# A hybrid encoder layer on one core: V's class transfers issued by ScalarE, and the product groups that stand beside the attention spread anew

## The chip, the core and the metric

The kernel runs on 1 core of one Trainium2 chip. The metric is the device time of one execution in microseconds (us), smaller being better. Inside a core, TensorE (PE) multiplies matrices into PSUM, VectorE (DVE) and ScalarE (ACT) do elementwise work, GpSimd (POOL) does small work and issues some transfers, and SyncE (SP) issues most transfers. Each engine takes its instructions in order; an instruction that waits holds up all that stand behind it on its engine.

## The reference

One layer with sequence 512 and width 1024, all in float32. Two head groups share one input projection: a gated linear recurrence (RG-LRU, forward and backward) and attention with three dilated windows. Cut to what matters here:

```python
h = rms_norm(x, attn_norm_g[l])
xr, gate, q, k, v = split(h @ w_in[l])              # 5 x 512 columns
y_rnn = (rg_lru(xr, fwd) + rg_lru(xr, bwd)) * gelu(gate)
y_attn = dilated_attention(q, k, v, rel_bias)       # 8 heads of 64; windows (128,1), (512,4), (2048,16)
mix = concat([rms_norm(y_rnn, g1), rms_norm(y_attn, g2)])
x = x + mix @ w_out[l]
x = x + square(relu(rms_norm(x, g3) @ w_up[l])) @ w_down[l]
return rms_norm(x, final_norm_g)
```

## The kernel before, in words

Every large product is made of three matmuls in a reduced float32 format (`mm3`, L311): the high part of the weights with the high and the low part of the data, and the low part of the weights with the high part of the data. A **group** below is one `mm3` over a contraction of 128. Weights come in chunks of 512 KB into three buffers (`wraw`). For each chunk ACT makes the high part (`conv_hi`, L260) and DVE the low part (`conv_lo`, L268); the low part frees the buffer, and `emit_dma` (L243) asks SP for the next chunk. In the Q and K products `feed_q` does this for the chunk three ahead, the high part at contraction step k = 1 and the low part at k = 5.

The order of work on PE, ACT, DVE and POOL is written out by hand: it is the order of the program. Only SP's order is found by the framework, from readiness in its own model.

The stages that matter here: V is projected early and stays in PSUM; ACT writes it to SBUF during the gate products (`v_evac`, L717). `v_far(j)` (L722) then copies V from SBUF to SBUF in another order, by classes of positions modulo 4: five transfers in all, 256 KB each but two of 128 KB, from 128 partitions into 32 (16) each. The result `vc` is read by `att_av`, first at the end of step 1.

Then comes the attention: five steps i = 0 to 4, each of four quarters u = 0 to 3. Step i treats head pair p = i (i < 4) and finishes pair i - 1:

- `att_s(i, 0)` and `att_s(i, 2)`: scores on PE, near (`pn`, L777) and far (`pf`, L784). The near ones have two PSUM buffers, so `att_s(i, 2)` waits until DVE has read those of quarters 0 and 1. Scores need `qraw` (L749), `kraw` (L753) and, for the far ones, `kfar`, K rearranged by ACT (`k_far`, L757).
- `att_f` (L797) and `att_e` (L816, L819): bias and minimum on DVE, exponential on ACT.
- `att_t` (L831, L833): transposes on PE, evacuated by ACT; `att_r`: the same for the reciprocal denominators.
- `att_av(i - 1)` (L912): the product with V at the end of the step, evacuated by DVE (`yp`, L928), then squared on ACT and added on DVE (`att_y`, L588).

Between these pieces stand **fillers**, groups of other products, taken in order from a queue by `fill(n)`: first 48 groups for K and Q of pairs 1 to 3 (8 for K, 8 for Q of each pair), then `load_x`, then 32 groups of the recurrence half of the output projection (`wo_thunks`, `pwo<-whi,yh`). Six are taken ahead of step 0 (`PRE`), then `FILL[(i, u)]` says how many at each of the four places of a quarter, four in all where it has no entry. `plan` hangs further pieces of ACT and DVE work on such places (`beside(i, u, place)`).

`load_x` reuses the two buffers of the normed input, so it starts when the last K or Q group is done. It loads the residual `x1` and four sums of blocks of w_out (`ws`): a plain load by SP (L1001) and then accumulating loads by POOL (L1003), each of which waits for the one before on the same sum.

Behind step 4: `att_av(3)`, `att_y(3)`, a few fillers, the column sums of the squares (`col_sums`, L411), `rv` (DVE, L396), `rcol`, the reciprocal root (POOL, L399), the remaining fillers, and the attention half of the output projection by a seven-product scheme of half blocks (`wo_m`, `pwo<-whi,oh`, in the order of `OSEQ`), whose results DVE scales by `rcol` and adds to `x1` (`wo_x`, L1120). The recurrence half is evacuated by DVE in L967. The up and down projections follow and take the larger part of the time.

Of the kernel before, what the change touches and what calls it, by code (L numbers as in the profile page):

```python
# [108 lines left out]
def hybrid_kernel(ctx: ExitStack, tc, xw, xn, w_in, w_v, w_out, w_up, w_dn, gates, vecs, rel, onehot, fg, out):  # L109
    nc = tc.nc  # L110
# [12 lines left out]
    def g_(name, dt=FT, shape=(P, S)):  # L123
        return work.tile(list(shape), dt, name=name, tag="g", bufs=NG)
# [4 lines left out]
    def ps_(name, tag):  # L129
        return psum.tile([P, S], FT, name=name, tag=tag, bufs={"pj": 4, "gs": 2, "et": 2}[tag])  # L130
# [122 lines left out]
    def conv_hi(i):  # L253
        if i < len(chunks):
            i = swap.get(i, i)
            hi = stream.tile([P, 1024], FR, name="whi", tag="whi", bufs=4)
            if i in ON_DVE:
                nc.vector.tensor_copy(hi, raws[i])
            else:
                act(hi, raws[i], AF.Copy)  # L260
            splits[i] = (hi,)

    def conv_lo(i):
        if i < len(chunks):
            i = swap.get(i, i)
            r = raws.pop(i)
            lo = stream.tile([P, 1024], FR, name="wlo", tag="wlo", bufs=4)
            nc.vector.tensor_tensor(lo, r, f(splits[i][0]), op=OP.subtract)  # L268
            splits[i] += (lo,)
            c = chunks[i]  # L270
            if isinstance(c, tuple) and c[0] == "o":
                if c[1][0] != "s":
                    emit_dma()
            elif isinstance(c, tuple) and len(c) == 4:
                h, kind, f0 = c[:3]
                if kind == "t1" and cq[h, f0, "t2"] not in raws:
                    nc.gpsimd.dma_start(r, ublock(h, "22", f0), accum_op=OP.add)
                    raws[cq[h, f0, "t2"]] = r
                elif kind == "22":
                    t = raws[cq[h, f0, "t3"]]  # L280
                    nc.vector.tensor_tensor(t, t, r, op=OP.add)
                elif kind in ("t2", "21"):
                    held[kind] = r
                    if len(held) == 2:
                        t = held.pop("t2")
                        nc.vector.tensor_tensor(t, t, held.pop("21"), op=OP.add)
                        raws[cq[h, f0, "t4"]] = t
                        emit_dma()
                if kind in ("11", "22"):
                    emit_dma()  # L290
            elif isinstance(c, tuple) and c[1][0] == "s":
                nxt = {"s1": ("s2", "22"), "s2": ("s4", "21")}.get(c[1])
                if nxt:
                    nc.gpsimd.dma_start(r, wblock(c[0], nxt[1], c[2]), accum_op=OP.add)
                    raws[cd_[c[0]] + {"s2": 2 * NQ + 2 * c[2], "s4": 6 * NQ + c[2]}[nxt[0]]] = r
            else:
                emit_dma()
# [7 lines left out]
    def feed_q(c, k):  # L305
        if k == 1:
            conv_hi(c + 3)
        elif k == 5:
            conv_lo(c + 3)

    def mm3(o, a, b, first, last, on=False):  # L311
        nc.tensor.matmul(o, lhsT=a[0], rhs=b[0], start=bool(first), stop=False, skip_group_check=on)  # L312
        nc.tensor.matmul(o, lhsT=a[0], rhs=b[1], start=False, stop=False, skip_group_check=on)  # L313
        nc.tensor.matmul(o, lhsT=a[1], rhs=b[0], start=False, stop=bool(last), skip_group_check=on)  # L314
# [60 lines left out]
    def hk(k):  # L375
        return (h_hi[:, k, :], h_lo[:, k, :])

    def wk(c, k):
        if c < 3:
            return tuple(t[:, c * P:(c + 1) * P] for t in w3[k])  # L380
        hi, lo = splits[c]
        return (hi[:, k * P:(k + 1) * P], lo[:, k * P:(k + 1) * P])
# [144 lines left out]
    def lru_gelu(t):  # L527
        act(gt[t], gt[t], AF.Gelu_apprx_tanh)
# [182 lines left out]
    vs, vc = vb[:, 0:4, :], vb[:, 4:8, :]  # L711
# [7 lines left out]
    def v_far(j):  # L719
        for a, b, s in (((0, P, 32 * j - 16),) if j else ((0, 64, 112), (64, P, 0))):  # L720
            n = (b - a) // 4
            nc.sync.dma_start(vc[s:s + n], vs[a:b, j, :])  # L722

    last = [scan_ops_end(t) for t in range(4)]

# [29 lines left out]
    def k_far(p):  # L755
        t = raw[p, 2] = g_("kfar")
        act(t.rearrange("p (c s) -> p s c", c=4), raw[p, 1].rearrange("p (s c) -> p s c", c=4), AF.Copy)  # L757
# [82 lines left out]
    def att_z(p):  # L840
        rz = small("rz", 8)
        nc.vector.reciprocal(rz, zs.pop(p))
        rzb = g_("rzb")
        nc.vector.tensor_copy(rzb, fan(rz, 0, 8, DH))
        rzbs[p] = rzb

    def att_r(p):
        rzb = rzbs.pop(p)
        pr = rows_of(lambda tt: rzb[:, tt * P:(tt + 1) * P], "et")
        zrow[p] = g_("zrow")  # L850
        act(zrow[p], pr, AF.Copy)
# [81 lines left out]
    def q_thunks(p, is_k, tag="pj"):  # L933
        c = C_QK + 2 * p + 1 - is_k
        o = {}

        def mk(k):
            def run():
                if k == 0:
                    o["p"] = ps_("pqk", tag)  # L940
                mm3(o["p"], wk(c, k), hk(k), k == 0, k == KD - 1)
                feed_q(c, k)
                if k == KD - 1:
                    (k_evac if is_k else q_evac)(p, o["p"])
            return run
        return [mk(k) for k in range(KD)]
# [23 lines left out]

    for n, th in enumerate(q_thunks(0, 1) + q_thunks(0, 0)):
        th()
        if n == 8:
            k_far(0)
        if n % 4 == 0:
            lru_gelu(n // 4)
    fillers = deque()

    def fill(n):
        for _ in range(n):  # L980
            if fillers and fillers[0] is None:
                fillers.popleft()
                load_x()
            if fillers:
                fillers.popleft()()
# [25 lines left out]
    def hi(t):  # L1011
        return lambda: y_hi(t, yrnn[t])

    def lo(t):
        return lambda: y_lo(t, yrnn.pop(t))

    def end(t):
        return lambda: rnn_end(t)

    def sq_(t):  # L1020
        return lambda: rnn_sq(t)
# [4 lines left out]
    def op(fn, *a):  # L1026
        return lambda: fn(*a)


    plan = {(0, 0, 0): [end(0)], (0, 0, 2): [sq_(0), add], (0, 0, 3): [end(1)],  # L1030
            (0, 1, 1): [sq_(1)],
            (0, 2, 3): [add],
            (1, 0, 2): [end(2)],
            (1, 1, 0): [sq_(2)], (1, 1, 2): [end(3)], (1, 1, 4): [add],
            (1, 3, 0): [sq_(3)], (1, 3, 2): [hi(0)], (1, 3, 3): [add, hi(1)], (2, 0, 2): [rnn_cols],
            (2, 0, 0): [lo(0), lo(1)], (2, 0, 4): [hi(2)],
            (2, 1, 2): [hi(3)], (2, 1, 4): [lo(2)], (2, 2, 3): [lo(3)]}
    for i in range(3):
        plan.setdefault((i, 1, 0), []).append(lambda p=i + 1: k_far(p))

    def beside(*key):
        for e in plan.pop(key, ()):
            e()
# [5 lines left out]
    for key, fs in (((4, 0, 4), [(o_sum, "s1", 0), (o_sum, "s2", 0), (o_sum, "s3", 0), (o_sum, "s3", 1)]),  # L1049
# [2 lines left out]
                    ((4, 2, 0), [(o_hi, "s3", 0), (o_hi, "s3", 1)]), ((4, 2, 2), [(o_lo, "s3", 0), (o_lo, "s3", 1), (o_sum, "22", 0)]),  # L1052
                    ((4, 2, 4), [(o_hi2, 0)]), ((4, 3, 0), [(o_lo2, 0), (o_hi, "s1", 0)]), ((4, 3, 4), [(o_lo, "s1", 0), (o_hi, "22", 0), (o_lo, "22", 0)])):
        plan[key] = [op(*a) for a in fs]
    FILL = {(3, 1): (1, 1, 1, 0), (3, 2): (1, 1, 1, 0), (3, 3): (1, 1, 1, 0), (4, 0): (0, 1, 0, 0), (4, 1): (0, 1, 0, 1), (4, 2): (0, 1, 0, 0), (4, 3): (0, 0, 0, 1)}


    for i in range(5):
        for u in range(4):
            if i == 0:  # L1060
                v_far(u)
            if i < 4 and u in (0, 2):
                att_s(i, u)
                if i < 3:
                    load_tw(2 * i + 2 + u // 2)
            if i >= 1 and u < 3:
                att_t(2 * i - 2, "abc"[u])
                att_t(2 * i - 1, "abc"[u])
            if i < 4:
                if u < 2:  # L1070
                    att_f(i, 2 * u)
                    att_f(i, 2 * u + 1)
                att_e(i, u)
            if u == 0 and i >= 1:
                att_z(i - 1)
            beside(i, u, 0)
            fill(FILL.get((i, u), (1, 1, 1, 1))[0])
            beside(i, u, 1)
            fill(FILL.get((i, u), (1, 1, 1, 1))[1])
            if u == 1 and i >= 1:  # L1080
                att_r(i - 1)
            if u == 0 and i >= 2:
                att_y(i - 2)
            beside(i, u, 2)
            fill(FILL.get((i, u), (1, 1, 1, 1))[2])
            beside(i, u, 3)
            fill(FILL.get((i, u), (1, 1, 1, 1))[3])
            beside(i, u, 4)
            if u == 3 and 1 <= i < 4:
                att_av(i - 1)  # L1090
    assert not plan
# [43 lines left out]
    def h2_l(k):  # L1135
        nc.vector.tensor_tensor(hb["l"][:, k, :], hm[k], f(hb["h"])[:, k, :], op=OP.subtract)

    fill(1)
    att_av(3)
    att_y(3)  # L1140
    fill(4)
    cs = col_sums(ssy[1], "gs")
    rc[1] = rstd_cols(cs, S)
    o_sum("s1", 1)
# [17 lines left out]
    for w in OSEQ:  # L1162
        for i in range(4):
            tt, k = (i % 2, i // 2) if w == "s2" else (i // 2, i % 2)
# [253 lines left out]
    for half in range(2):  # L1418
# [202 lines left out]
        if half == 1:  # L1621
            b = 6 * NQ
# [87 lines left out]
```

## Time and profile before

| | us |
|---|---|
| median of 3 runs | 538.83 (537.76 to 539.11) |
| the profiled execution | 539.04 |
| its span | 537.2 |
| PE busy | 524.9 |
| DVE busy | 423.3 |
| ACT busy | 352.2 |
| POOL busy | 64.0 |

The span is the time from the first to the last instruction of the profiled execution; 1.8 us lie around it. In a row of the timeline the columns are the start, the duration, the engine and its line, the operation, the output and the inputs, and the count; a bracket holds the idle time of the engine just before and what ended it. The ends of matmuls are modelled, so PE's rows overlap. The attention runs from 97.9 us to the column sums at 187.3 us; the up projection begins at 212.8 us.

### The profile page before, as it was taken

How to read it: one execution, taken by the hardware profiler on the slowest of the kernel's cores; microseconds unless marked ns; L12 is line 12 of the kernel's file. 1: busy time of each engine (PE TensorE's matmuls, PEld its weight loads, DVE VectorE, ACT ScalarE, POOL GpSimd, SP SyncE). 2: the span in 40 equal slices, each digit the busy share in tenths (PEclk: the TensorE clock that was granted, in tenths of full speed). 3: DMA queues.
4: the chain of work that ended last, by engine and by line, in shares of the span. 5: the costliest groups of instructions: out<-in, count | busy, mean ns of one | idle time of the engine just before them, and what ended most of it. 6: DMA issues, size and time to landing. Idle time of an engine off the chain costs nothing.

```text
span 537.2 us, 9162 instructions
## 1 busy us (share of the span) xinstructions
PE 524.9 (98%) x3507; PEld 448.3 (83%) x3507; DVE 423.3 (79%) x695; ACT 352.2 (66%) x557; POOL 64.0 (12%) x91
## 2 busy tenths in 40 slices
PE   8999999899999999999999999999999999999995
PEld 6866888687887778889999888888999999888884
DVE  6897787776674799889769987879756987987885
ACT  7677957567845745586576755566657686655664
POOL 3330000000001130001030213001001110131000
PEclk9999999999999999999999999999999999999998
DMA  7754068642299688856586799995888496799704
GB/s 276 210 161 141 32 171 182 183 114 70 90 298 307 165 166 203 285 193 180 166 177 177 195 252 274 288 356 116 282 235 206 117 220 193 174 301 263 174 0 157
DMA packets 34587, 104.10 MB, mean 194 GB/s; under 512 B 3981, under 2 KB 6954, under 8 KB 34544
## 3 DMA queue, kind: packets, MB, share of 16 engines
q1 hardware_dynamic: 26304, 74.66, 41.2%
q0 software_dynamic: 7920, 28.61, 28.5%
q8 instruction: 27, 0.44, 0.4%
q10 hardware_dynamic: 320, 0.25, 0.1%
q14 instruction: 16, 0.13, 0.1%
HBM read 96.15 MB, written 4.21 MB: 187 GB/s over the span
## 4 chain that ended last, share of the span: by engine, by line
PE 75%; DMA 10%; ACT 5%; DVE 5%; issue 2%; POOL 1%; SPq 0%; DVEq 0%; ACTq 0%; POOLq 0%
PE pu L314 10%; PE pu L313 10%; PE pu L312 10%; PE pd L312 9%; PE pd L314 9%; PE pd L313 9%; DMA ws<-in_w_out_dram 6%; DMA wraw<-in_w_in_dram 3%; PE pqk L312 2%; PE pqk L313 1%; PE pqk L314 1%; PE pg L502 1%; PE pxr L312 1%; PE pxr L314 1%; PE pxr L313 1%
## 5 line engine op out<-in xcount | busy, mean ns | idle before, releaser
L268 DVE TENSOR_TENSOR wlo<-wraw,whi 128x1024 fp32r<-128x1024 f32 x73 | 88.9, 1221 | 28.3 <-ACT whi L260 28.1
L260 ACT ACTIVATE whi<-wraw 128x1024 fp32r<-128x1024 f32 x70 | 74.0, 1059 | 44.6 <-PE pd L314 20.5
L313 PE MATMUL pd<-wlo,ah 128*128 128x512 f32 (+1 forms) x195 | 75.2, 386 | 0.0
L312 PE MATMUL pd<-whi,ah 128*128 128x512 f32 (+1 forms) x195 | 75.2, 386 | 0.0
L314 PE MATMUL pd<-whi,al 128*128 128x512 f32 (+1 forms) x195 | 75.2, 386 | 0.0
L313 PE MATMUL pu<-hl,whi 128*128 128x256 f32 x224 | 63.4, 283 | 0.0
L314 PE MATMUL pu<-hh,wlo 128*128 128x256 f32 x224 | 63.4, 283 | 0.0
L312 PE MATMUL pu<-hh,whi 128*128 128x256 f32 x224 | 63.4, 283 | 0.0
L260 ACT ACTIVATE whi<-tw 128x1024 fp32r<-128x1024 f32 x36 | 38.1, 1060 | 37.0 <-DMA tw<-in_w_up_dram 10.1
L314 PE MATMUL pu<-h2h,wlo 128*128 128x256 f32 (+1 forms) x200 | 60.1, 301 | 0.2 <-DVE wlo L268 0.2
L312 PE MATMUL pu<-h2h,whi 128*128 128x256 f32 (+1 forms) x200 | 60.1, 300 | 0.0
L313 PE MATMUL pu<-h2l,whi 128*128 128x256 f32 (+1 forms) x200 | 60.0, 300 | 0.0
L268 DVE TENSOR_TENSOR wlo<-tw,whi 128x1024 fp32r<-128x1024 f32 x36 | 44.0, 1222 | 17.5 <-ACT whi L260 17.5
L312 PEld LDWEIGHTS pu<-hh,whi 128*128 128x128 f32 x224 | 43.0, 192 | 0.0
L313 PEld LDWEIGHTS pu<-hl,whi 128*128 128x128 f32 x224 | 43.0, 192 | 0.0
L314 PEld LDWEIGHTS pu<-hh,wlo 128*128 128x128 f32 x224 | 43.0, 192 | 0.0
L314 PEld LDWEIGHTS pd<-whi,al 128*128 128x128 f32 x195 | 36.6, 188 | 7.4
L313 PEld LDWEIGHTS pd<-wlo,ah 128*128 128x128 f32 x195 | 36.6, 188 | 7.4
L312 PEld LDWEIGHTS pd<-whi,ah 128*128 128x128 f32 x195 | 36.6, 188 | 7.2
L260 ACT ACTIVATE whi<-ts 128x1024 fp32r<-128x1024 f32 x24 | 25.5, 1061 | 24.3 <-PE pd L314 18.1
L314 PEld LDWEIGHTS pu<-h2h,wlo 128*128 128x128 f32 x200 | 38.3, 191 | 1.8 <-DVE wlo L268 0.6
L312 PEld LDWEIGHTS pu<-h2h,whi 128*128 128x128 f32 x200 | 38.3, 191 | 1.3
(265 smaller groups left out, 1222.6 us busy)
## 6 DMA issues: line engine op xcount, KB each, us to landing
wraw<-in_w_up_dram SPq DMA_DIRECT2D x25, 512.0 KB
ts<-in_w_dn_dram POOLq DMA_DIRECT2D x24, 512.0 KB, 13.6
wraw<-in_w_dn_dram SPq DMA_DIRECT2D x24, 512.0 KB
tw<-in_w_up_dram SPq DMA_DIRECT2D x15, 512.0 KB
tw<-in_w_up_dram POOLq DMA_DIRECT2D x15, 512.0 KB, 7.4
wraw<-in_w_in_dram SPq DMA_DIRECT2D x13, 512.0 KB
ts<-in_w_dn_dram SPq DMA_DIRECT2D x8, 512.0 KB
tw<-in_w_dn_dram SPq DMA_DIRECT2D x8, 512.0 KB
```

The source lines that it names most:

```text
L260: act(hi, raws[i], AF.Copy)
L268: nc.vector.tensor_tensor(lo, r, f(splits[i][0]), op=OP.subtract)
L312: nc.tensor.matmul(o, lhsT=a[0], rhs=b[0], start=bool(first), stop=False, skip_group_check=on)
L313: nc.tensor.matmul(o, lhsT=a[0], rhs=b[1], start=False, stop=False, skip_group_check=on)
L314: nc.tensor.matmul(o, lhsT=a[1], rhs=b[0], start=False, stop=bool(last), skip_group_check=on)
L502: nc.tensor.matmul(pg[2 * d + j][halves[b ^ d]], lhsT=gwr[t][halves[b], c], rhs=xc[t][halves[b]], start=True, stop=True)
```

## The change

`v_far` issues its transfers on ACT's queue in place of SP's, and in step 0 it is called at the end of each quarter in place of its beginning. `k_far(p)` is called by the third Q group of its pair, in place of fixed places (the ninth group of the first pair's products, and the second quarter's start of steps 0 to 2).

The filler table changes. Steps 0 to 2 take 14 groups each (4, 3, 4, 3 by quarter) in place of 16; step 3 takes 12 in place of 13; step 4 takes 8 in place of 5. So the 48 K and Q groups end with step 2, where before six groups of the output projection had been taken by then. 20 of the 32 groups of the output projection are taken by the end of step 4, before 24. None is now taken between step 4 and `att_av(3)`, before one; five stand between `att_y(3)` and the column sums, before four; and seven behind them, before three.

```diff
     def v_far(j):
         for a, b, s in (((0, P, 32 * j - 16),) if j else ((0, 64, 112), (64, P, 0))):
             n = (b - a) // 4
-            nc.sync.dma_start(vc[s:s + n], vs[a:b, j, :])
+            nc.scalar.dma_start(vc[s:s + n], vs[a:b, j, :])
...
                 mm3(o["p"], wk(c, k), hk(k), k == 0, k == KD - 1)
                 feed_q(c, k)
+                if k == 2 and not is_k:
+                    k_far(p)
...
     for n, th in enumerate(q_thunks(0, 1) + q_thunks(0, 0)):
         th()
-        if n == 8:
-            k_far(0)
...
-    for i in range(3):
-        plan.setdefault((i, 1, 0), []).append(lambda p=i + 1: k_far(p))
...
-    FILL = {(3, 1): (1, 1, 1, 0), (3, 2): (1, 1, 1, 0), (3, 3): (1, 1, 1, 0), (4, 0): (0, 1, 0, 0), (4, 1): (0, 1, 0, 1), (4, 2): (0, 1, 0, 0), (4, 3): (0, 0, 0, 1)}
+    FILL = {(i, u): (1, 1, 1, 1 - u % 2) for i in range(3) for u in range(4)}
+    FILL.update({(3, u): (1, 1, 1, 0) for u in range(4)})
+    FILL.update({(4, u): (0, 1, 0, 1) for u in range(4)})
...
     for i in range(5):
         for u in range(4):
-            if i == 0:
-                v_far(u)
...
             beside(i, u, 4)
+            if i == 0:
+                v_far(u)
             if u == 3 and 1 <= i < 4:
                 att_av(i - 1)
...
-    fill(1)
     att_av(3)
     att_y(3)
-    fill(4)
+    fill(5)
```

## The prediction

> **What bounds the kernel now.** I read the page first (busy times), then busy time by stage for the attention and what follows it (columns after the stretch: length, busy time and count of PE, PEld, DVE, ACT, POOL, then clock, DMA share, GB/s), then the timeline of each engine where PE pauses.
>
> ```profile
> span 537.2 us, 9162 instructions
> PE 524.9 (98%) x3507; PEld 448.3 (83%) x3507; DVE 423.3 (79%) x695; ACT 352.2 (66%) x557; POOL 64.0 (12%) x91
> 100.00:113.90 13.90, 12.56 (x80) 9.40 (x80) 12.62 (x46) 9.61 (x22) 0.00 (x0) 1.00 0.33 99
> 113.90:133.80 19.90, 19.90 (x240) 15.69 (x240) 13.22 (x48) 13.69 (x30) 0.00 (x0) 1.00 0.32 90
> 133.80:154.60 20.80, 20.80 (x246) 16.56 (x244) 13.93 (x49) 13.72 (x30) 2.04 (x2) 1.00 0.47 158
> 154.60:172.40 17.80, 17.80 (x229) 14.00 (x227) 9.39 (x43) 10.65 (x26) 2.68 (x3) 1.00 1.05 311
> 172.40:187.30 14.90, 13.66 (x93) 10.21 (x91) 11.18 (x22) 10.09 (x21) 2.65 (x3) 1.00 0.71 180
> 187.30:197.20 9.90, 8.94 (x41) 6.87 (x41) 9.19 (x17) 4.33 (x7) 2.93 (x3) 1.00 0.91 167
> ```
>
> The six stretches are attention steps i = 0 to 3, then step 4, then the start of the attention half of the output projection. TensorE sets the time, at full clock. Steps 1 to 3 have no PE pause at all, so nothing can be gained there. The pauses are in step 0, in step 4 and behind it: 1.34 + 1.24 + 0.96 us. No PE work is added or dropped, only moved, so the change is worth what it does to these pauses. They are, on PE:
>
> ```profile
> 82.53 0.39 PE L312 MATMUL pqk<-h_hi,whi 128*128 128x512 f32 x1
> 97.26 0.39 PE L314 MATMUL pqk<-h_hi,wlo 128*128 128x512 f32 x1
> 97.89 1.09 PE L777 MATMUL pn<-kraw,qraw 64*32 64x192 f32 x32 [0.25 <-DVE qraw L749]
> 99.84 0.50 PE L312 MATMUL pqk<-h_hi,whi 128*128 128x512 f32 x1
> 105.19 0.39 PE L314 MATMUL pqk<-h_hi,wlo 128*128 128x512 f32 x1
> 106.92 1.39 PE L777 MATMUL pn<-kraw,qraw 64*32 64x256 f32 x32 [1.34 <-DVE mn L816]
> 108.24 0.50 PE L312 MATMUL pqk<-h_hi,whi 128*128 128x512 f32 x1
> 175.52 1.15 PE L831 MATMUL pt<-ident,e 128*128 128x128 f32 x8 [0.41 <-ACT ett L833]
> 187.28 1.05 PE L411 MATMUL pcs<-ones,ysq 128*128 128x1 f32 x8 [0.16 <-DVE ysq L588]
> 190.35 0.39 PE L312 MATMUL pwo<-whi,oh 128*128 128x512 f32 x1
> 193.84 0.50 PE L312 MATMUL pwo<-whi,oh 128*128 128x512 f32 x1 [0.60 <-DVE x L1120]
> 197.23 0.50 PE L312 MATMUL pwo<-whi,oh 128*128 128x512 f32 x1 [0.38 <-DVE x L1120]
> ```
>
> The first two rows are the first and the last of 66 matmuls in a row, so 14.73 / 65 = 0.227 us each, and a product group (three) costs **0.68 us**. A matmul's shown end is 0.16 us beyond that pace, so a pause is really about 0.16 us longer than its bracket.
>
> **Part 1: V's class transfers go from SP to ACT, and later.**
>
> ```profile
> SPq L722 <- ACT vs L717: 7.7, 3, 3.8
> 85.58 1.74 SPq L722 DMA_DIRECT2D vs<-vs  x2
> 87.44 0.52 SPq L243 DMA_DIRECT2D wraw<-in_w_in_dram  x1
> L722 SPq DMA_DIRECT2D vs<-vs x5: 597/610/669, 79.8 to 97.3; - x5
> 98.38 1.06 ACT L260 ACTIVATE whi<-wraw 128x1024 fp32r<-128x1024 f32 x1 [2.27 <-DMA wraw<-in_w_in_dram]
> 99.47 1.23 DVE L268 TENSOR_TENSOR wlo<-wraw,whi 128x1024 fp32r<-128x1024 f32 x1 [1.63 <-ACT whi L260]
> 100.61 0.28 DVE L797 CUSTOM_DVE_ANT_0 e<-pf,tw 128x128 f32<-128x128 f32 x1
> ```
>
> SP is one ordered queue. It stood 7.7 us at the class transfers until ACT had written V, with weight chunks queued behind them (the chunk at 87.44 follows the pair at 85.58 at once), and the transfers themselves then run beside those chunks. So a chunk lands late, ACT converts it only at 98.38 after 2.27 us of waiting, and DVE's low part runs at 99.47 to 100.70, while the far scores are already done (PE goes on to other work at 99.84). That holds up the first softmax piece, 100.61, and with it everything up to the score matmuls that wait at 106.92: 6.31 us of DVE back to back (DVE 12.62 of 13.90 us). With SP free I expect the low part done before the scores. Also qraw, which held PE for 0.25 us (0.3 by the pace), is no longer queued behind a late conversion. The first piece then starts at about 99.84 - 0.3 + 0.1 = 99.65, so DVE is 0.96 us earlier.
>
> ACT pays five issues of 0.61 = 3.1 us in step 0, where it is busy 9.61 of 13.90 us: 4.3 us are free, and each issue comes after the last group of a quarter step. What is queued behind them on ACT are the exponentials and two conversions; PE waits on ACT's results there only a step later. I take 0, bounds 0 and +3.1. SP saves the same 3.1 us, worth nothing more. The K rearrangements (kfar) move by at most three groups, ahead of their use in the next step: 0.
>
> The row says that what counted was the place in the queue. The Trainium skill, "DMA: Bandwidth & Descriptors", section "Issuing engines are not separate DMA queues", holds that transfers from any issuer share the same 16 engines and that issuing elsewhere saves only initiation time, usually small. By it alone the move is worth nothing, and part 1 is then rival D; no run so far separates the two.
>
> **Part 2: fewer groups per step.** Step 0 has one group fewer ahead of the waiting scores. PE leaves them at 108.24 - 0.96, with one group (0.68) less done: net **-0.28 us**. Bounds: +0.68 if DVE is no earlier, -1.6 if both of step 0's pauses go.
>
> ```profile
> 121.48 0.48 DVE L816 CUSTOM_DVE_ANT_0 e<-pn,tw,mf 128x256 f32<-128x256 f32 x1
> 123.61 0.99 PE L777 MATMUL pn<-kraw,qraw 64*32 64x256 f32 x32
> 147.65 0.33 SPq L1001 DMA_DIRECT2D ws<-in_w_out_dram  x1
> 151.86 2.82 PE L912 MATMUL pav<-ett,vs 128*64 128x128 f32 x32
> 154.61 0.99 PE L777 MATMUL pn<-kraw,qraw 64*32 64x192 f32 x32
> ```
>
> Step 1: the same wait has 123.61 - 121.96 = 1.65 us of slack. One group less takes 0.68, and since the groups now run two behind, a low part (1.23) slips into the DVE chain: -0.26. **+0.2**, bounds 0 and +0.7. Steps 2 and 3: DVE is busy 13.93 of 20.80 and 9.39 of 17.80 us, so 0, bounds 0 and +0.7 each. Step 4 has two fillers per quarter: the 0.41 at 175.52 waits on ACT's evacuation, and one more group covers it, **-0.5** (bounds 0 and -0.6). At the column sums, 187.28, five groups in place of four cover the square and its addition: **-0.3** (0.16 + 0.16; bounds 0 and -0.3). Sum up to here: -0.88, so the attention half of the projection, which all groups precede as before, starts at 189.47 in place of 190.35.
>
> **Part 3: the end.** Seven groups in place of three stand between the column sums and that start. Rows for what they cover:
>
> ```profile
> 184.29 1.77 POOL L1003 DMA_DIRECT2D ws<-in_w_out_dram  x2 [5.25 <-DMA ws<-in_w_out_dram]
> 190.13 1.15 POOL L399 TENSOR_TENSOR rcol<-rv,mhalf 128x4 f32<-128x4 f32 x1 [4.06 <-DVE rv L396]
> 189.89 0.15 DVE L396 TENSOR_SCALAR rv<-pcs 128x4 f32<-128x4 f32 x1
> 191.39 1.41 DVE L967 SCALAR_TENSOR_TENSOR x<-pwo,rcol,x 128x512 f32<-128x512 f32 x2
> 193.04 1.40 DVE L1120 SCALAR_TENSOR_TENSOR x<-pwo,rcol,x 128x512 f32<-128x512 f32 x2
> 194.36 1.21 DVE L268 TENSOR_TENSOR wlo<-ws,whi 128x1024 fp32r<-128x1024 f32 x1
> 195.50 0.68 DVE L881 TENSOR_TENSOR ol<-at,oh 128x512 fp32r<-128x512 f32 x1
> 196.10 0.41 DVE L897 SCALAR_TENSOR_TENSOR osum<-osum,at 128x256 f32<-128x256 f32 x1
> ```
>
> The column sums come four groups (2.72) and 0.88 us earlier, at 183.68. But the reciprocal root (rcol) is on POOL behind the accumulating loads of w_out, whose issues end at 184.29 + 1.77 = 186.06 and had 4.06 us to spare. They start when the last K/Q group is done (147.65). That group now ends step 2, and only the 2.75 us of the value matmuls (151.86 to 154.61) follow it: 154.61 - 6 x 0.68 - 0.28 + 0.2 - 2.75 = 147.7. So the loads do not move, and POOL, not rv, is last: rcol is done at about 187.3 (before: 191.28). DVE then owes its negative (0.2), four evacuations of 0.70 (before, two), a low part (1.15), a short low part (0.35) and the first L1120 (0.70): 5.2 us, 192.5. PE is through the first product's four groups at 189.47 + 2.73 = 192.2 and waits 0.3 there. The next release takes DVE 0.70 + 1.15 + 0.6 + 0.35 + 0.70 = 3.5 us more, 196.0 against PE's 197.23 before. (Check on before: 193.04 + 0.70 + 3.5 = 197.24.) Sum: **-1.2 us**. Behind 197.23 DVE and PE keep their old order and distance, and nothing later changes.
>
> The profiled execution took 539.04 us (span 537.2), so 537.8. The median of the runs, 538.83, is 0.2 lower: **537.6 us**. About 0.3%, 1.6 us, is what a measurement of this kernel can tell from no change, and the forecast is inside it, at -0.22%.
>
> **The rivals**, each from the sum -1.2. The forecast itself, between 536.6 and 538.6, has 0.34.
>
> A, the end opens more (0.22): rcol early, because the loads of w_out finish sooner, and step 0's wait shrinks. POOL's end at 185 or earlier gives 0.5 us more until PE's own start binds; half of step 0's remaining 1.0 us does the rest: -2.2, **536.6**. For: the groups at the end are more than the pauses there. Against: DVE is 9.19 of 9.90 us busy there.
>
> B, the attention's own chain becomes the bound (0.14): each of steps 1 to 3 pays a whole group, 2.04 us in place of 0.2: +0.6, **539.4**. For: step 1 misses by 0.26. Against: idle DVE in steps 2 and 3.
>
> C, the loads of w_out end later (0.11), the slower case: the bias tiles come free earlier, so the next up-projection loads (two of 512 KB) get in front of load_x on SP. At the 311 GB/s of the saturated stretch (share 1.05) that is 3.4 us for rcol, which has no slack left, and DVE and PE follow one for one: -1.2 + 3.4 = +2.2, **541.0**. It loses from 1.2 us of delay on. Against: those loads share the stretch already.
>
> D, the class transfers were not what made the chunk late (0.12), so step 0 is +0.68: -0.2, **538.6**.
>
> E, ACT's 3.1 us are exposed (0.07), since the exponentials come late and the transposes of step 1 wait: +1.9, **540.7**.
>
> **Numbers.** Faster by over 0.3%: A, and 0.13 of the forecast's 0.34, whose spread crosses 537.2: 0.35. Slower: C and E, 0.18. Same: 0.47. The range takes A with step 0 at its bound, and E: 535.9 to 540.7, leaving out C's centre and the tails. The forecast's own range is 536.6 to 538.6.
>
> **What would show it.** On ACT five issues in step 0 and no wait of the conversion near 98 for its chunk; DVE's first e piece within 0.2 us of the far scores' end; the (0,2) score wait still over 1 us; no PE pause at the column sums; rcol released by POOL's own loads, not by rv; the two pauses at L1120 together near 0.8 in place of 0.98. Wrong if the loads of w_out end more than 1 us away from 186, if steps 1 to 3 show PE pauses beyond 0.3 us each, or if PE waits on exponentials.

## The result, and the profile after

The changed kernel takes **541.8 us** (median of 7 runs, 541.14 to 543.63) against 538.83 for the kernel before (7 runs on the same chip): a ratio of 1.0058, 95% interval 1.0039 to 1.0077. It is slower, where the forecast said 537.6 and the range ended at 540.7. The profiled execution took 541.14 us, with a span of 539.2, against 539.04 and 537.2. So the two traces show 2 us of the 3.0 between the medians; what makes up the rest stays open.

The page of the changed kernel begins:

```profile
span 539.2 us, 9166 instructions
PE 525.2 (97%) x3507; PEld 448.6 (83%) x3507; DVE 423.8 (79%) x695; ACT 351.6 (65%) x557; POOL 64.8 (12%) x91
```

The work is the same, as expected. What has to be found is 2 us of idle PE. These are PE's pauses in the changed kernel, step 0 to the third product of the attention half, from PE's timeline, with the starts of steps 1 to 3, of the value matmuls and of the column sums between them (these rows hold only the first matmuls of their group):

```profile
105.76 1.39 PE L777 MATMUL pn<-kraw,qraw 64*32 64x256 f32 x32 [1.34 <-DVE mn L816]
112.07 0.39 PE L777 MATMUL pn<-kraw,qraw 64*32 64x192 f32 x8
123.91 0.66 PE L831 MATMUL pt<-ident,e 128*128 128x128 f32 x4 [1.25 <-ACT zrow L851]
132.05 0.39 PE L777 MATMUL pn<-kraw,qraw 64*32 64x192 f32 x8
151.49 0.39 PE L777 MATMUL pn<-kraw,qraw 64*32 64x192 f32 x8
169.97 0.66 PE L831 MATMUL pt<-ident,e 128*128 128x128 f32 x4 [0.67 <-DVE rz L842]
178.25 0.33 PE L912 MATMUL pav<-ett,vs 128*64 128x128 f32 x2
184.53 0.39 PE L411 MATMUL pcs<-ones,ysq 128*128 128x1 f32 x3
191.75 0.47 PE L312 MATMUL pwo<-whi,oh 128*128 128x512 f32 x1 [1.35 <-DVE x L969]
195.86 0.47 PE L312 MATMUL pwo<-whi,oh 128*128 128x512 f32 x1 [0.73 <-DVE x L1119]
199.25 0.47 PE L312 MATMUL pwo<-whi,oh 128*128 128x512 f32 x1 [0.38 <-DVE x L1119]
```

Beside the rows of before, the pauses at `qraw`, at step 4's evacuation (175.52) and at the column sums are gone; the 0.67 us on `rz` were there before (173.76). Two are new: 1.25 us in step 1, on ACT, and 1.35 us at the first product of the attention half, on DVE. The third product starts at 199.25 against 197.23: +2.02 us, the whole difference of the spans. So the search ends there. (L969, L1119 and L1145 are L967, L1120 and L1147 of before.)

DVE, which holds PE at 191.75, is itself waiting. From the waits between 184 and 200 us (line, releaser, total, times, longest):

```profile
DVE nrc L1145 <- POOL rcol L399: 4.2, 1, 4.2
```

And from the timelines of DVE, POOL and SP (SPq is SP issuing a transfer, and so are POOL's rows at L1003):

```profile
185.63 0.15 DVE L396 TENSOR_SCALAR rv<-pcs 128x4 f32<-128x4 f32 x1
187.90 1.78 POOL L1003 DMA_DIRECT2D ws<-in_w_out_dram  x2 [6.09 <-DMA ws<-in_w_out_dram]
189.02 1.71 POOL L399 TENSOR_TENSOR rcol<-rv,mhalf 128x4 f32<-128x4 f32 x1
160.35 0.99 POOL L1003 DMA_DIRECT2D ws<-in_w_out_dram  x1 [20.70 <-DMA ws<-in_w_out_dram]
148.84 3.65 SPq L997 DMA_DIRECT2D x<-in_xn_dram  x8
152.53 4.02 SPq L1001 DMA_DIRECT2D ws<-in_w_out_dram  x4
```

Read from the wait on: DVE stands 4.2 us for `rcol`. Its input `rv` is there from 185.78, yet POOL computes `rcol` only at 189.02 to 190.73, because the last two accumulating loads stand ahead of it, and they waited 6.09 us for the landing of the loads before them. That chain begins with the plain loads on SP, and here they are issued from 152.53 on, behind all eight loads of x1. The kernel before had its first w_out load ahead of them:

```profile
148.07 3.85 SPq L997 DMA_DIRECT2D x<-in_xn_dram  x8
151.59 0.99 POOL L1003 DMA_DIRECT2D ws<-in_w_out_dram  x1 [10.51 <-DMA ws<-in_w_out_dram]
162.24 2.68 POOL L1003 DMA_DIRECT2D ws<-in_w_out_dram  x3 [9.66 <-DMA ws<-in_w_out_dram]
```

With its first load at 147.65 (shown with the prediction), the chain was 4.9 us ahead at the first plain load, 8.8 at the first accumulating one, and 3.6 at the last pair (184.29 against 187.90). No line of `load_x` was edited. SP's order is the framework's, and it came out otherwise here. What had changed around it is the place of the last K and Q group, which frees the two buffers; why the framework then chose as it did, no run settles.

The new pause in step 1 is on ACT. The changed kernel, then the kernel before, from ACT's timeline:

```profile
120.61 0.62 ACT L819 ACTIVATE e<-e,mn 128x384 f32<-128x384 f32 x1 [1.28 <-DVE mn L816]
121.82 0.61 ACT L582 ACTIVATE ysq<-gt 128x512 f32<-128x512 f32 x1
122.34 1.04 ACT L260 ACTIVATE whi<-wraw 128x1024 fp32r<-128x1024 f32 x1
123.29 0.57 ACT L851 ACTIVATE zrow<-prow 128x512 f32<-128x512 f32 x1
```

```profile
118.50 1.05 ACT L260 ACTIVATE whi<-wraw 128x1024 fp32r<-128x1024 f32 x1
124.27 0.65 ACT L851 ACTIVATE zrow<-prow 128x512 f32<-128x512 f32 x1
```

The conversion of a weight chunk hangs on a group. With the groups further behind, it moved from 118.50, ahead of the exponentials of 121.60, to 122.34, between those and `zrow`, and PE's transposes wait for `zrow`.

### The profile page after: what moved, and what is told of

It reads as the page before. It is cut to its first block, busy times and chain, and to the rows that moved or that the text cites. A ratio compares the mean times of both kernels' runs of the same rounds, so it can differ in the third digit from the quotient of the medians.

```text
span 539.2 us, 9166 instructions
## 1 busy us (share of the span) xinstructions
PE 525.2 (97%) x3507; PEld 448.6 (83%) x3507; DVE 423.8 (79%) x695; ACT 351.6 (65%) x557; POOL 64.8 (12%) x91
## 4 chain that ended last, share of the span: by engine, by line
PE 83%; DMA 7%; DVE 5%; issue 1%; ACT 1%; SPq 1%; POOL 1%; DVEq 0%; POOLq 0%; ACTq 0%
PE pu L314 10%; PE pu L312 10%; PE pu L313 10%; PE pd L314 9%; PE pd L312 9%; PE pd L313 9%; DMA ws<-in_w_out_dram 6%; PE pqk L312 2%; PE pqk L314 2%; PE pqk L313 2%; PE pg L502 2%; PE pv L312 2%; PE pv L314 1%; PE pv L313 1%; PE pp L314 1%; PE pp L312 1%
## 5 line engine op out<-in xcount | busy, mean ns | idle before, releaser
L313 PEld LDWEIGHTS pu<-h2l,whi 128*128 128x128 f32 x200 | 38.3, 191 | 1.3
```

## The experiments

**1. The w_out loads ahead of x1's.** The changed kernel, with the two loops of `load_x` exchanged:

```diff
+        ws = big.tile([P, 4, 1024], FT, name="ws", tag="bigB")
+        for i, (n, bs) in enumerate(...):          # plain and accumulating loads of w_out
+            ...
         for n in range(2):
             for g in range(4):
                 x1[g, n] = xb[:, 2 * g + n, :]
                 nc.sync.dma_start(x1[g, n], xn[2 * g + n])
-        ws = big.tile([P, 4, 1024], FT, name="ws", tag="bigB")
-        for i, (n, bs) in enumerate(...):
-            ...
```

> The changed kernel, with one edit: load_x asks for the four plain loads of w_out's sums before the eight loads of x1, so SP issues them first. Theory 1 (the loss is the chain of accumulating loads of w_out on POOL, which starts later because SP now issues the eight x1 loads, 3.7 us, ahead of it, and which holds rcol): the first accumulating load issues about 3.5 us sooner, rcol ends near 187.5 in place of 190.7, the first pwo<-whi,oh matmul near 190.1 in place of 191.75, and the time is 2.3 to 3.0 us under the changed kernel's, 538.8 to 539.5. Theory 2 (the loss lies in the attention steps, where PE now pauses 1.25 us in step 1 behind ACT, and in the groups moved to the end): this edit moves rcol but the time by less than 0.5 us, 541.3 to 542.

Measured: 538.97 us, ratio to the kernel before 1.0002 (0.9987 to 1.0018). The loss is gone. SP, POOL and PE:

```profile
148.92 1.75 SPq L997 DMA_DIRECT2D ws<-in_w_out_dram  x4
185.82 1.77 POOL L999 DMA_DIRECT2D ws<-in_w_out_dram  x2 [5.31 <-DMA ws<-in_w_out_dram]
186.94 1.71 POOL L399 TENSOR_TENSOR rcol<-rv,mhalf 128x4 f32<-128x4 f32 x1
124.24 0.66 PE L831 MATMUL pt<-ident,e 128*128 128x128 f32 x4 [1.24 <-ACT zrow L851]
193.77 0.47 PE L312 MATMUL pwo<-whi,oh 128*128 128x512 f32 x1 [0.31 <-DVE x L1119]
```

`rcol` ends at 188.65 in place of 190.73, the pause at the first product is gone, and step 1's pause is still there. The up-projection load (145.32) and a weight chunk (148.43) still go ahead of the w_out loads: it was x1's eight loads that cost.

**2. `rcol` ahead of the last two accumulating loads**, SP's order left as the change has it: those two loads are issued behind `rstd_cols` in the program.

```diff
-                nc.gpsimd.dma_start(t, oblock(b), accum_op=OP.add)
+                if (n, b) in (("s4", "21"), ("s1", "12")):
+                    late.append((t, b))
+                else:
+                    nc.gpsimd.dma_start(t, oblock(b), accum_op=OP.add)
...
     rc[1] = rstd_cols(cs, S)
+    for t, b in late:
+        nc.gpsimd.dma_start(t, oblock(b), accum_op=OP.add)
```

> The changed kernel, with one edit: the last two accumulating loads of w_out's sums (the fourth block of s4 and the second of s1) are issued by POOL behind rcol, not ahead of it; everything else as in the changed kernel, the late chain too. Theory 1 in its narrow form (rcol standing in POOL's queue behind these two issues is what costs): rcol ends near 187, DVE is not held at nrc for 4.2 us, the pause of 1.35 us at the first pwo<-whi,oh goes; the late sum s4 (193.2) still holds ACT, so about 1.5 to 2 us are won, 539.8 to 540.3. In its wide form (the sum s4 itself arrives too late for its conversion, whatever rcol does): 0 to 0.5 us won, 541.3 to 541.8. Theory 2: no change, 541.5 to 542.

Measured: 539.67 us, 1.0015 (0.9998 to 1.0031). From POOL and PE:

```profile
186.07 1.14 POOL L399 TENSOR_TENSOR rcol<-rv,mhalf 128x4 f32<-128x4 f32 x1 [3.98 <-DVE rv L396]
188.30 1.83 POOL L1148 DMA_DIRECT2D ws<-in_w_out_dram  x2 [1.08 <-DMA ws<-in_w_out_dram]
198.07 0.47 PE L312 MATMUL pwo<-whi,oh 128*128 128x512 f32 x1 [1.56 <-DVE x L1124]
```

`rcol` now waits for `rv`, not for the loads, and most of the loss goes with that alone: it was POOL's queue. The loads are as late as they were, so the products that use the last two sums pay: 1.56 us at the third product. (The profiled execution took 540.23 us, and its third product starts 1.18 us earlier than the changed kernel's, so the trace shows about half of the gain of the medians.)

**3. The class transfers back on SP**, the rest of the change kept.

```diff
-            nc.scalar.dma_start(vc[s:s + n], vs[a:b, j, :])
+            nc.sync.dma_start(vc[s:s + n], vs[a:b, j, :])
...                                                 # and v_far(u) at the quarter's beginning again
```

> The changed kernel with the class transfers of V put back on SP at the beginning of each quarter of step 0, the fillers as changed. If moving them is a gain of its own (DVE's first softmax piece waits for a late chunk again), step 0 is 0.9 to 1.1 us longer and with it the last K/Q group and the chain of loads: 542.5 to 543.0. If ACT's five issues cost time (the rival), it is faster than the changed kernel by up to 1 us, 540.8. If the transfers are hidden either way: 541.5 to 542.

Measured: 542.3 us, 1.0061 (1.0042 to 1.008): the same as the changed kernel. In its trace the first softmax piece starts at 99.70, in time although the transfers are on SP. From this I formed the idea that the later `k_far` was already a cure for step 0, which experiment 10 tests.

**4. The class transfers on ACT and nothing else**: the first and the last hunk on `v_far`, in the kernel before.

> The kernel before with the class transfers of V alone changed (on ACT, at the end of each quarter of step 0), fillers and K rearrangements as before. If the move is a gain of its own: DVE's first softmax piece starts near 99.6 in place of 100.6, PE's pauses at 97.9 and 106.9 lose 0.9 to 1.1 us together, 537.7 to 538.0. If ACT's issues cost: up to 1 us slower, 539.8. If hidden either way: 538.6 to 539.0.

Measured: 537.88 us, 0.9976 (0.9959 to 0.9992): faster. The rows that answer part 1:

```profile
94.12 1.04 ACT L260 ACTIVATE whi<-wraw 128x1024 fp32r<-128x1024 f32 x1
99.88 0.29 DVE L797 CUSTOM_DVE_ANT_0 e<-pf,tw 128x128 f32<-128x128 f32 x1 [2.87 <-PE pf L784]
106.20 1.39 PE L777 MATMUL pn<-kraw,qraw 64*32 64x256 f32 x32 [0.66 <-DVE mn L816]
```

The conversion runs at 94.12, before at 98.38, without a wait for its chunk; DVE waits for the scores instead of the scores for DVE, and the pause at (0, 2) is 0.66 in place of 1.34 us. That the move gains is told by the medians, not by this trace: in that of experiment 7, where the transfers are on SP as in the kernel before, the first piece starts at 99.64 and the pause is 0.78 us.

**5. Experiment 1 and step 1's groups 3, 4, 4, 3** by quarter in place of 4, 3, 4, 3.

```diff
+    FILL.update({(1, 0): (1, 1, 1, 0), (1, 1): (1, 1, 1, 1)})
```

> The kernel of the first experiment (changed, with the loads of w_out's sums first), and the fillers of step 1 dealt 3, 4, 4, 3 to the quarters in place of 4, 3, 4, 3. The conversion that stood ahead of the zrow evacuation on ACT then comes behind it, and one group more stands ahead of the transposes. Theory (with the late loads gone, what is left between forecast and result is PE's pause of 1.24 us at the transposes of step 1): the pause goes, PE is 1.0 to 1.4 us earlier, 537.6 to 538.0, ratio near 0.998. Rival (what PE gains there is lost again at the end, where rcol still waits for POOL's loads): DVE waits longer at nrc, and the time stays at 538.6 to 539.2.

Measured: 537.27 us, 0.9981 (0.997 to 0.9992). The pause at `zrow` is gone, and `rcol` starts at 185.71, 1.2 us earlier than in experiment 1.

**6. Experiment 5 and `rcol` ahead of the last two loads.**

> The kernel of the fifth experiment, and rcol ahead of the last two accumulating loads on POOL as in the second. If rcol behind POOL's loads is what holds the end once the chain starts on time, rcol ends about 1.5 us sooner than with the loads ahead of it, and both pauses at the L1120 evacuations together fall under 1 us: 537.0 to 537.7. If DVE's own work or the arrival of the sum s4 holds it: no better than the fifth, within 0.3 us of it.

Measured: 536.98 us, 0.9969 (0.9957 to 0.9981): faster than both kernels, by 0.3% and 0.9%. From experiment 5 it isn't told apart.

**7. The kernel before, with the w_out loads ahead of x1's.**

> The kernel before with the loads of w_out's sums asked for ahead of those of x1. There SP already issued the first of the four ahead of x1, and rcol had 4.06 us to spare on POOL. If that slack is real, the earlier chain is worth nothing: 538.5 to 539.0, unless the later x1 loads hold DVE's first L967 (up to 0.5 us slower). If the chain bounds the kernel before too, it gains 0.5 us or more.

Measured: 540.2 us, 1.0037 (1.0019 to 1.0056), a miss. DVE and PE:

```profile
155.03 0.75 DVE L967 SCALAR_TENSOR_TENSOR x<-pwo,rcol,x 128x512 f32<-128x512 f32 x1 [4.62 <-DMA x<-in_xn_dram]
156.83 0.66 PE L831 MATMUL pt<-ident,e 128*128 128x128 f32 x4 [0.69 <-DVE yp L928]
```

The kernel before takes six groups of the output projection already in step 2, and the evacuation of the first result needs x1. It waits 4.62 us (before: 0.37), with `yp`, which PE needs, queued behind it. And an earlier chain gains nothing there, since `rcol` waited for `rv` anyway. The changed kernel takes none of these groups before step 3, so for it the same exchange is free. (The profiled execution took 539.13 us. At the start of step 3 it is 0.97 us ahead of the kernel before, 153.64 against 154.61, since its step 0, with the same program, went quicker; at the third product it is 0.05 ahead, 197.18 against 197.23. So this trace shows a loss of 0.9, the medians 1.5.)

**8. The kernel before with the class transfers on ACT, the w_out loads first, and `rcol` ahead of the last two loads.**

> The kernel before with the class transfers on ACT (as in the fourth experiment), the loads of w_out's sums ahead of x1, and rcol ahead of the last two accumulating loads. With the fillers as before rcol waits for rv and not for POOL, so nothing is expected beyond the fourth experiment: 537.6 to 538.1. If the chain of loads matters there too, 537.0 to 537.5.

Measured: 544.52 us, 1.0119 (1.01 to 1.0139), a miss, and a clear one:

```profile
157.79 0.66 PE L831 MATMUL pt<-ident,e 128*128 128x128 f32 x4 [1.56 <-DVE yp L928]
191.04 1.14 POOL L399 TENSOR_TENSOR rcol<-rv,mhalf 128x4 f32<-128x4 f32 x1 [13.86 <-DVE rv L396]
192.16 1.81 POOL L1150 DMA_DIRECT2D ws<-in_w_out_dram  x2
201.45 0.50 PE L312 MATMUL pwo<-whi,oh 128*128 128x512 f32 x1 [3.69 <-DVE x L1125]
```

The first row is experiment 7's wait, here 1.56 us. The larger loss is at the end: POOL stands 13.86 us at `rcol`, and the loads behind it, which went nearly 8 us earlier in the kernel before (184.29), come late: PE waits 3.69 us behind the work on what they bring. In this kernel `rv` comes only at 191, since the column sums come later, with three groups behind them and not seven. One queue, both ways: whichever of the two is ready first must stand first.

**9. Step 1's groups alone**: the changed kernel with the one line of experiment 5, SP's order left.

> The changed kernel with step 1's groups taken 3, 4, 4, 3 by quarter in place of 4, 3, 4, 3; nothing else. Theory 1 (the late w_out loads bind the end, and they start one for one with the last K/Q group, so step 1's 1.25 us pause is a part of the loss): the pause at the transposes of step 1 goes, x1's loads and the w_out loads start about 1.2 us earlier, rcol ends near 189.5 in place of 190.7, and the time is 540.4 to 540.8 against 541.8. Rival, the loads are bound by what stands ahead of them on SP (the weight chunk of w_out at 148.13 and the up-projection load), not by the last K/Q group: the pause goes, rcol stays at 190.7, PE waits 1.2 us more at the attention half's start, and the time stays at 541.5 to 542.0.

Measured: 539.58 us, 1.0022 (1.0014 to 1.0031): 1.9 us by the ratios, where 1.0 to 1.4 were expected. SP and POOL:

```profile
147.74 3.81 SPq L997 DMA_DIRECT2D x<-in_xn_dram  x8
151.59 3.12 SPq L1001 DMA_DIRECT2D ws<-in_w_out_dram  x4
188.28 1.71 POOL L399 TENSOR_TENSOR rcol<-rv,mhalf 128x4 f32<-128x4 f32 x1
```

x1's loads start 1.1 us earlier (148.84 in the changed kernel), the w_out loads 0.9 and `rcol` 0.7. So step 1's pause reaches the end through the last K and Q group and the start of `load_x`. What PE itself gains is spent waiting for the same loads: its pause at the first product grows from 1.35 to 1.71 us, and the third product starts at 198.51, 0.74 earlier, as much as `rcol` gained. The medians show more than that, 1.9, and why stays open (the span is 1.3 us shorter, but 0.6 of that lies behind PE's last matmul).

**10. `k_far` alone**: the kernel before, with only the K rearrangements moved.

> The kernel before with only the rearrangements of K moved to the third Q group of their pair; V's class transfers stay on SP. Theory 1 (the conversion at 98.38 was late through two things in series, the place of its chunk's load behind the class transfers on SP and the rearrangement ahead of ACT's conversions, and either cure is enough): the conversion of the last chunk ahead of step 0 runs near 97.5, the first softmax piece starts near 99.7 as with the transfers moved, and the time is 537.7 to 538.2, the same as with the transfers moved alone (537.9). Rival, only the transfers' place made the chunk late: conversion near 98.4, first piece near 100.6, and the time is that of the kernel before, 538.6 to 539.1.

Measured: 538.66 us, 1.0006 (0.9994 to 1.0018): nothing. My theory of two causes in series fell, and the time is the rival's. ACT and SP, from an execution of 540.07 us, above the median:

```profile
95.45 1.06 ACT L260 ACTIVATE whi<-wraw 128x1024 fp32r<-128x1024 f32 x1 [4.31 <-DMA wraw<-in_w_in_dram]
99.26 1.06 ACT L260 ACTIVATE whi<-wraw 128x1024 fp32r<-128x1024 f32 x1 [1.28 <-DMA wraw<-in_w_in_dram]
90.21 7.92 SPq L243 DMA_DIRECT2D wraw<-in_w_in_dram  x3
```

The last chunk is as late as ever (99.26), and it is the transfer, not the rearrangement, that ACT waits for.

**11. Experiment 6 with the class transfers back on SP**, where no late load covers step 0.

> The best version so far (w_out loads ahead of x1's, step 1's groups 3, 4, 4, 3, rcol ahead of the last two accumulating loads; 536.98), with V's class transfers back on SP at the quarters' starts. Here no late load hides what step 0 is worth. Theory 1 (SP's place ahead of the weight chunks is what makes the last chunk late, whatever else is changed): the conversion ahead of step 0 runs after 98, the first softmax piece starts near 100.6, and the time is 537.7 to 538.1, the 0.9 that the move alone brought. Rival (with the K rearrangement behind the conversion the chunk comes in time from SP as well): the first piece starts near 99.7 and the time is 536.8 to 537.3.

Measured: 537.43 us, 0.9981 (0.9965 to 0.9997), between the two expectations; the runs lie between 536.12 and 540.83, those of experiment 6 between 536.45 and 537.36. The intervals of the two overlap, so what the move is worth in this surrounding, 0.45 us by the medians, isn't settled. The profiled execution took 536.12 us, so its trace tells how it can go, not how it mostly does:

```profile
91.31 1.06 ACT L260 ACTIVATE whi<-wraw 128x1024 fp32r<-128x1024 f32 x1 [1.60 <-DMA wraw<-in_w_in_dram]
88.78 5.20 SPq L243 DMA_DIRECT2D wraw<-in_w_in_dram  x3
```

**12. Experiment 6 with step 0's groups 4, 4, 3, 3**, one more ahead of the scores that wait.

```diff
-    FILL.update({(1, 0): (1, 1, 1, 0), (1, 1): (1, 1, 1, 1)})
+    FILL.update({(0, 1): (1, 1, 1, 1), (0, 2): (1, 1, 1, 0), (1, 0): (1, 1, 1, 0), (1, 1): (1, 1, 1, 1)})
```

> The best version so far with step 0's groups taken 4, 4, 3, 3 by quarter in place of 4, 3, 4, 3, so that one group more stands ahead of the scores that wait 1.34 us on DVE. Theory 1 (this pause is PE time lost on the path, and DVE's chain ahead of it doesn't move): the pause falls to 0.66, step 1 has its old slack, and the time is 536.2 to 536.5 against 536.98. Rival: the extra group's weight chunk is converted earlier on DVE, inside the softmax chain, or the pause comes back at the start of step 1, where the last two quarters now have one group fewer: 536.9 to 537.4.

Measured: 536.9 us, 0.9963 (0.9949 to 0.9977). The pause fell as expected, and no other took its place up to the third product of the attention half:

```profile
106.23 1.39 PE L777 MATMUL pn<-kraw,qraw 64*32 64x256 f32 x32 [0.67 <-DVE mn L816]
195.12 0.47 PE L312 MATMUL pwo<-whi,oh 128*128 128x512 f32 x1 [0.49 <-DVE x L1125]
```

That product starts 0.83 us earlier than in experiment 6 (195.95), and PE's last matmul 0.80 earlier (528.15 against 528.95), but the span is only 0.2 shorter: from that matmul to the end there are 7.05 us here and 6.45 there (6.96 in the changed kernel). Whether this spread of the last stretch hides a true gain isn't settled by one trace of each. Experiments 6 and 12 are the quickest versions by their medians, and not told apart.

## Why the prediction was wrong

Up to the attention half, step by step. A step's net is the shift of its end against before, less 0.68 us for each group that it has more or fewer:

| | predicted | measured | worked out |
|---|---|---|---|
| step 0 | -0.28 | -0.47 | 112.07 - 113.90 + 2 x 0.68 |
| step 1 | +0.2 | **+1.46** | (132.05 - 133.78) + 1.83 + 1.36 |
| step 2 | 0 | -0.03 | (151.49 - 154.61) + 1.73 + 1.36 |
| steps 3 and 4 | -0.5 | -0.67 | (178.25 - 181.36) + 3.12 - 0.68 |
| column sums | -0.3 | -0.32 | (184.53 - 187.28) + 3.11 - 0.68 |
| sum | -0.88 | -0.03 | |
| from there to the third product | -0.3 | **+2.05** | 199.25 - 197.23 + 0.03 |

Two of the prediction's own signs of being wrong came true: the loads' issues end at 189.68 and not near 186, and step 1 has a PE pause of 1.25 us.

**Part 1 was right in its time, and its mechanism is half shown.** Five issues on ACT cost PE nothing there, the conversion no longer waits for its chunk, and the first piece starts at 99.44 in the changed kernel (predicted 99.65). Alone it brought 0.8 us by the medians, 0.4 to 2.2 by the interval (experiment 4; 0.96 predicted, on DVE), and rival D falls with that for the kernel before; with the rest of the change around it, its worth stays between 0 and that (experiments 3 and 11). The prediction's reading that "what counted was the place in the queue" is not shown, since the change moves the issuer and the time together: the class transfers are issued from 79.8 to 97.3 us in the kernel before, among the weight chunks, and from 103.1 to 111.6 in experiment 4, behind them. The late chunk is issued 1.55 us earlier there (88.44 against 89.99), which is its place on SP, but converted 4.26 us earlier (94.12 against 98.38). From its issue to its conversion pass 6.96 to 9.05 us in the five traces with the class transfers on SP, and 5.34 to 5.68 in the nine with them on ACT. So the larger part is a quicker arrival without the class transfers beside it. Class transfers issued late by SP were not run, so what ACT as the issuer is worth stays open. The rule weighed there, from the Trainium skill's "DMA: Bandwidth & Descriptors", section "Issuing engines are not separate DMA queues", speaks of initiation time; as the transfers were also moved in time, experiment 4 does not go against it, and no run here tests it alone. "K rearrangements: 0" was right too (experiment 10). Rival E falls: step 1's pause on ACT is the same with the transfers on SP (1.24 us, experiment 3), and with them on ACT alone there is none (experiment 4).

**Part 2 failed at step 1**, "+0.2, bounds 0 and +0.7". Its slack was taken from one wait, the scores' on DVE, and a conversion was looked for on DVE only. The same chunk has a high part on ACT, and that slipped between the exponentials and `zrow`: +1.46 (experiments 5 and 9 take the pause away). The wait for `zrow` had no slack in the kernel before: `zrow` ends at 124.92 there, and the four transposes that need it were due at about 124.96 (an estimate, half of the way from 124.53 to 125.38). So the group that is missing counts in full, 0.68, and `zrow` ends 0.77 us later after the step's start (123.86 - 112.07 against 124.92 - 113.90); no run changes one of the two alone. Rival B, a whole group lost in each step, is half of what happened in step 1, and in steps 2 and 3 nothing of it did. Steps 0 and 4 and the column sums came out within 0.2 us.

**Part 3 failed at "So the loads do not move".** The release was computed well enough: 147.7 forecast, x1's loads at 148.84, and step 1's error alone is 1.26 us of delay. But the order behind the release was taken from before, and there the first w_out load went ahead of x1's eight by the framework's choice. Behind them, it starts at 152.53. From there the rest of part 3 is right in kind: POOL's loads, not `rv`, are last, and DVE and PE follow `rcol`. It ends at 190.73 in place of 187.3, 3.4 us late, and the sum of this part is +2.05 in place of -0.3. Experiments 1 and 2 show it from two sides: mend SP's order or POOL's, and 3.0 or 2.3 us by the ratios (1.0058 to 1.0002 and 1.0015) come back, 2.0 and 1.0 by the spans of the traces.

Rival C, "the loads of w_out end later", 541.0, named the right victim and nearly the right time, with a chance of 0.11. That the time was so near is luck, for its cause was another, up-projection loads in front: with one such load and a weight chunk still ahead, experiment 1 is as quick as the kernel before. The two errors are not independent, since step 1's delay also starts the loads later: mending the one brought 1.9 us (experiment 9), the other 3.0, and both 4.1 (experiment 5), all by the ratios to the kernel before.

## What to carry to other kernels

Where a scheduler chooses one queue's order, a change that moves a buffer's release can reorder that queue without touching it: ask not only when a transfer is released, but what is released with it and which goes first. When a piece of work slides along one engine's list, follow its parts on every engine, since 0.2 us had been booked for DVE's low part, and the step cost 1.46 with the high part on ACT. And where loads and a small operation on the path share an in-order queue, what is ready first must stand first: the same exchange gained 2.3 us in one kernel (experiment 2) and was part of a loss of 5.8 us in another (experiment 8).

## What the runs showed of the hardware

A transfer beside others has no fixed length from one execution to the next. With the class transfers on SP, the issues of three weight chunks behind them, each of which waits for a buffer and so for a landing, spanned 7.22 us in the kernel before (89.99 to 97.21) and 5.84 in experiment 7, which are one program up to there, and 5.74, 7.92 and 5.20 in experiments 3, 10 and 11, which are one program up to there too. In the traces of 3, 7 and 11 the chunk was in time, or nearly, with the transfers on SP. So one trace of such a kernel shows one draw, and experiment 3, whose trace was of a good one, led me to a cause that experiment 10 then refuted.

A lead is not kept along a chain of loads: 4.9 us at the first plain load were 8.8 us at the first accumulating one and 3.6 us at the last pair. In between lies a stretch in which the 16 DMA engines were always busy. From the busy time by stage of the changed kernel, for step 3 (length, busy time and count of PE, PEld, DVE, ACT and POOL, then clock, DMA share, GB/s):

```profile
151.49:168.64 17.15, 17.15 (x226) 13.43 (x225) 10.44 (x44) 10.51 (x26) 0.99 (x1) 1.00 1.03 354
```

The reciprocal root on POOL showed 1.71 us wherever it stood directly behind accumulating loads (the changed kernel, experiments 1 and 9) and 1.14 where it had waited for `rv` (experiments 2 and 8). I had booked 1.15. Behind the loads its record begins before that of their issue ends (189.02 against 189.68 in the changed kernel), so the longer one may hold some waiting; no run here separates the two.
